# Weighing two heads instead of three on TensorE in most units of a mixture of softmaxes, with a new order of instructions

## The chip, the core and the metric

The kernel runs on one core of one Trainium2 chip. The metric is the device time of one execution in microseconds (us), lower is better. A core has five engines that run side by side, each working through its own instructions in order: TensorE (PE in the profile) multiplies matrices into PSUM, VectorE (DVE), ScalarE (ACT) and GpSimd (POOL) work on 128 partitions at a time, and SyncE (SP) here only issues DMAs. Sixteen DMA engines move data between HBM and SBUF.

## The reference: what is computed

```python
logits: (32, 128, 4 heads, 4096) float32; prior: (32, 128, 4) float32
prior_probs = softmax(prior, axis=-1)              # over the 4 heads
softmax     = softmax(logits, axis=-1)             # over the 4096 columns
mixture     = sum over heads of prior_probs * softmax   # (32, 128, 4096) float32
```

So 256 MiB are read, 64 MiB are written, and every logit is needed three times: for the maximum of its row, for the exponential and its sum, and for the weighted sum over the heads.

## The kernel before, in words

The work is cut into 32 **units** of 128 rows, one row to a partition. A unit has four heads of 128 x 4096 float32 (2 MB each). They are loaded into a **ring** of 11 slots of one head each (`slot`, line 104: head h of unit u sits in slot (4u + h) mod 11). A unit whose four heads run over the end of the ring is loaded by two DMAs, the others by one. The output is 2 MB a unit. It is put together in `obuf`, a single buffer, or from unit 24 on in some units in the slot of head 3 (`home`, line 107), and leaves from there.

Each step has a letter, and the order of the whole program is a hand-made text of such letters (`ORDER`), which `run` (line 193) turns into instructions. Each engine gets its instructions in that order and waits inside it; data dependencies between engines become semaphore waits. A word like `X0+1` means step X, argument 0, of the unit after the current one; `T12'` would be of the unit before; `@23` names the unit. Digits behind the head number are quarters of the 4096 columns: `12` is the second quarter (1024 columns), `24` the last two.

- `L` (`load`, line 112) and `S` (`store`, line 119): DMAs issued by SyncE, in one queue.
- `M` (`peak`, line 122, VectorE): minus the maximum of a head's rows.
- `E` (`exp`, line 127, ScalarE): the exponential in place, with the sum of each row.
- `R` (`recip`, line 133, VectorE): one over that sum.
- `G` (`diagonal`, line 136, GpSimd): the identity matrix times (one over the sum) times (prior weight), a 128 x 128 matrix.
- `X` (`weigh`, line 143, TensorE): that diagonal matrix times a head, added up in PSUM (`acc`, 4096 columns). A float32 block of 512 columns is two instructions in the trace, so a head is 16 of them.
- `C` (`weight`, line 152, GpSimd): the same weight as one number a row (`wght`).
- `Z` (`scale`, line 155, GpSimd): a head's columns times its weight, in place.
- `A`, `B`, `T` (`term`, line 162, VectorE): head times weight plus something else: plus `acc` into the output (`A`), plus `acc` into the head's own slot (`B`), head 3 plus what is in the slot of head 2 into the output (`T`, both from SBUF).
- `V` (`evac`, line 181, ScalarE): a quarter of `acc` copied into the slot of head 1.
- `P` (`add_scaled`, line 184, GpSimd): the slot of head 1 plus the slot of head 3, into the output.

In the **steady part** before (line 29, the first 23 entries of `ORDER`) TensorE weighs heads 0, 1 and 2 of each unit. Head 3 is finished in two ways: in the first half of the columns VectorE adds it to `acc` (`A01'`, `A12'`), in the second half ScalarE copies `acc` out (`V23'`, `V34'`), GpSimd scales head 3 (`Z324'`) and adds the two (`P23'`, `P34'`). These come behind the first maximum of the following unit. The store of a unit and the load two units further on are issued by SyncE after that, `S' L+2`. From unit 23 on an order of its own (lines 32 to 65) names every step of the **last units**, with heads split into quarters; there some quarters of head 2 are not weighed by TensorE (`BYPASS`, line 66) but scaled by GpSimd and added (`W`, line 177) to head 3.

What sets when a load can start is the ring: `L` of unit u+2 overwrites heads 1, 2 and 3 of unit u-1 and head 0 of unit u. What sets when a unit's output can be written is that the store of the unit before has left `obuf`.

Of the kernel before, what the change touches and what calls it, by code (L numbers as in the profile page):

```python
# [9 lines left out]
AF = mybir.ActivationFunctionType  # L10
# [12 lines left out]

FIRST = "L01 L12 L23 L34"
ORDER = []
ORDER += [
    "M0 E0 R3' C3' Z324' M1 R0 G0 A01' A12' V23' P23' V34' P34' E1 X0 S' L+2 M2 E2 R1 "
    "G1 X1 M3 E3 R2 G2 X2 "  # L30
] * 23
ORDER += [
    "M0@23 R3@22 E0@23 M2@23 Z324@22 C3@22 V34@22 R0@23 A12@22 G0@23 V23@22 P34@22 "
    "X034@23 E2@23 M1@23 X023@23 P23@22 X012@23 R2@23 E1@23 A01@22 G2@23 M3@23 X001@23 "
    "R1@23 E3@23 M1@24 G1@23 X123@23 S@22 X112@23 X101@23 M0@24 E1@24 L02@25 X201@23 "
    "X134@23 R3@23 E0@24 R1@24 Z324@23 M3@24 X234@23 X223@23 C3@23 G1@24 V34@23 X212@23 "
    "R0@24 V23@23 A01@23 P34@23 E3@24 A12@23 L24@25 G0@24 M2@24 P23@23 X034@24 X023@24 "
    "X012@24 M0@25 E2@24 X001@24 X101@24 S@23 R2@24 E0@25 R3@24 G2@24 X134@24 M1@25 "
    "Z324@24 X123@24 C3@24 X234@24 L02@26 R0@25 E1@25 M2@25 G0@25 X223@24 X112@24 "
    "V34@24 X201@24 M3@25 V23@24 P34@24 X212@24 E2@25 P23@24 X023@25 A01@24 L24@26 "  # L40
    "X034@25 E3@25 A12@24 X001@25 R2@25 R1@25 G2@25 M1@26 G1@25 X101@25 X012@25 X112@25 "
    "R3@25 E1@26 M0@26 Z324@25 X123@25 C3@25 S@24 X212@25 M2@26 E0@26 X201@25 X134@25 "
    "L02@27 X223@25 R0@26 E2@26 A12@25 G0@26 X234@25 A01@25 M3@26 X012@26 V23@25 "
    "X001@26 V34@25 P23@25 X034@26 R1@26 E3@26 P34@25 R2@26 L24@27 X023@26 M0@27 G1@26 "
    "G2@26 X123@26 X112@26 M1@27 E0@27 X134@26 X101@26 X201@26 S@25 R3@26 E1@27 R0@27 "
    "Z324@26 M2@27 X212@26 C3@26 G0@27 X223@26 L02@28 X234@26 V23@26 A01@26 E2@27 "
    "P23@26 X023@27 A12@26 M3@27 X012@27 V34@26 X001@27 P34@26 X034@27 R1@27 E3@27 "
    "R2@27 G1@27 Z234@27 X123@27 L24@28 G2@27 M0@28 X112@27 X101@27 X134@27 R3@27 E0@28 "
    "M1@28 C3@27 Z304@27 X202@27 S@26 V34@27 W34@27 X223@27 R0@28 E1@28 M2@28 G0@28 "
    "P34@27 X034@28 L01@29 V01@27 R1@28 M3@28 G1@28 E2@28 X001@28 P01@27 X101@28 L12@29 "  # L50
    "X134@28 V12@27 R2@28 Z224@28 M0@29 V23@27 X012@28 E3@28 P23@27 X023@28 L23@29 "
    "X112@28 P12@27 M1@29 E0@29 X123@28 G2@28 X201@28 L34@29 V23@28 X212@28 R0@29 R3@28 "
    "G0@29 M2@29 V34@28 Z314@28 X023@29 E1@29 X034@29 C3@28 S@27 W23@28 A01@28 E2@29 "
    "R1@29 X001@29 W34@28 M3@29 L01@30 G1@29 P23@28 X101@29 V12@28 R2@29 E3@29 X012@29 "
    "P12@28 X123@29 L12@30 G2@29 P34@28 X134@29 R3@29 M0@30 X201@29 V34@29 C3@29 "
    "Z304@29 X112@29 V01@29 L23@30 E0@30 X223@29 M1@30 Z234@29 X212@29 P01@29 L34@30 "
    "V23@29 R0@30 E1@30 G0@30 M2@30 P23@29 X001@30 X034@30 W34@29 L01@31 V12@29 X023@30 "
    "R1@30 E2@30 M3@30 G1@30 P12@29 X012@30 X101@30 P34@29 L12@31 X134@30 R2@30 E3@30 "
    "M0@31 G2@30 X123@30 Z234@30 X112@30 L23@31 V34@30 R3@30 E0@31 C3@30 X212@30 M1@31 "
    "Z314@30 X201@30 W34@30 L34@31 X223@30 V12@30 R0@31 A01@30 E1@31 G0@31 P12@30 "  # L60
    "X012@31 M2@31 X001@31 S@28 P34@30 V23@30 X034@31 R1@31 E2@31 M3@31 G1@31 P23@30 "
    "X023@31 X134@31 S@29 X123@31 R2@31 E3@31 G2@31 C2@31 B234@31 X101@31 B223@31 S@30 "
    "X201@31 R3@31 C3@31 T23@31 X112@31 T34@31 X212@31 A01@31 S23@31 A12@31 S34@31 "
    "S01@31 S12@31 "
]
BYPASS = {(27, 3), (28, 2), (28, 3), (29, 3), (30, 3), (31, 2), (31, 3)}


@with_exitstack
def kernel(  # L70
# [6 lines left out]
    nc = tc.nc  # L77
    U, P, H, V = logits.shape
# [4 lines left out]
    W = 512  # L83
    C = V // 4
# [11 lines left out]
    wght = cpool.tile([P, U, H], FP32, name="wght")  # L96
# [7 lines left out]
    def slot(u, h, a=0, b=4):  # L104
        return ring[:, (4 * u + h) % SLOTS, a * C : b * C]

    def home(u, a, b):
        if u >= U - 3 or u >= 24 and u % 2:
            return slot(u, 3, a, b)
        return obuf[:, a * C : b * C]  # L110
# [32 lines left out]
    def weigh(u, h, a=0, b=4):  # L143
        e = slot(u, h)
        for k in range(a * C // W, b * C // W):
            nc.tensor.matmul(  # L146
                acc[:, k * W : (k + 1) * W], lhsT=diag[:, u % 2, h],
                rhs=e[:, k * W : (k + 1) * W],
                start=h == 0, stop=h == H - 2 or (u, k * W // C) in BYPASS and h == H - 3,
            )  # L150

    def weight(u, h):
# [9 lines left out]
    def term(u, h, o, more, a, b):  # L162
        nc.vector.scalar_tensor_tensor(  # L163
            out=o, in0=slot(u, h, a, b), scalar=wght[:, u, h : h + 1], in1=more,
            op0=ALU.mult, op1=ALU.add,
        )
# [7 lines left out]
    def add_both(u, a, b):  # L174
        term(u, 3, home(u, a, b), slot(u, 2, a, b), a, b)

    def add_second(u, a, b):
        e = slot(u, 3, a, b)
        nc.gpsimd.tensor_add(e, e, slot(u, 2, a, b))  # L179

    def evac(u, a, b):
        nc.scalar.activation(slot(u, 1, a, b), acc[:, a * C : b * C], AF.Copy)  # L182
# [1 line left out]
    def add_scaled(u, a, b):  # L184
        nc.gpsimd.tensor_add(home(u, a, b), slot(u, 1, a, b), slot(u, 3, a, b))  # L185

    step = {
        "L": load, "S": store, "M": peak, "E": exp, "R": recip, "G": diagonal, "X": weigh,
        "C": weight, "Z": scale, "A": add_last, "B": add_head, "T": add_both, "V": evac,
        "P": add_scaled, "W": add_second,  # L190
    }

    def run(u, words):
        for w in words.split():
            op, digits, back, on, at = re.fullmatch(
                r"([A-Z])(\d*)('*)(?:\+(\d+))?(?:@(\d+))?", w
            ).groups()
            v = int(at) if at else u - len(back) + int(on or 0)
            if 0 <= v < U:
                step[op](v, *map(int, digits))  # L200

    with tc.manual_schedule():
        run(0, FIRST)
        nc.scalar.dma_start(out=pr, in_=prior)
        run(1, "L")

        nc.gpsimd.memset(ident, 1.0)
        nc.gpsimd.affine_select(
            out=ident, in_=ident, pattern=[[-1, P]], compare_op=ALU.is_equal, fill=0.0,
            base=0, channel_multiplier=1,  # L210
        )

        nc.vector.reduce_max(pmax, pr, axis=AX.X)  # L213
        nc.vector.tensor_sub(pr, pr, pmax.unsqueeze(2).to_broadcast([U, P, H]))  # L214
        nc.scalar.activation(pr, pr, AF.Exp)  # L215
        nc.vector.reduce_sum(pmax, pr, axis=AX.X)  # L216
        nc.vector.reciprocal(pmax, pmax)
        nc.vector.tensor_mul(  # L218
            pn.rearrange("k h r -> k r h"), pr, pmax.unsqueeze(2).to_broadcast([U, P, H])
        )  # L220
        for t in range(P // 32):
            nc.vector.transpose(  # L222
                pp[32 * t : 32 * (t + 1)], pn[:, :, 32 * t : 32 * (t + 1)]
            )

        for u, words in enumerate(ORDER):
            run(u, words)


# [28 lines left out]
```

## Time and profile before

| what | value |
|---|---|
| median of 3 runs | 787.25 us (786.92 to 787.46) |
| the profiled execution's own time | 787.27 us |
| its span (first to last instruction) | 785.5 us |
| granted TensorE clock, mean | 0.959 |
| DMA: bytes, mean rate | 335.89 MB, 428 GB/s |
| chain that ended last: DMA, PE, DVE | 50%, 29%, 12% |

The page gives for each engine its busy time and its share of the span, in a strip of 40 slices how busy it was over time, then the DMA queues, the chain of waits that ended last, and groups of equal instructions with their mean duration. A busy share of an engine says how much work it has; whether this work sets the time is told by what waited for what.

### The profile page before, as it was taken

The page shows a single profiled execution, that of the slowest core. Times are in us where ns is not written, and L with a number is a line of the kernel's source. Part 1 is how long each engine was busy: PE and PEld are TensorE (multiplying, and loading weights), DVE is VectorE, ACT ScalarE, POOL GpSimd, SP SyncE. Part 2 cuts the span into 40 slices and gives each one's busy share as a digit, 9 for nine tenths or more (in the row PEclk, how much of TensorE's full clock was granted, in tenths as well). Part 3 has the DMA queues.
Part 4 walks back from the last instruction along what each step waited for, and adds up shares of the span by engine and source line. Part 5 has one row for each costly group of instructions (what it writes and reads, how often), then busy time and mean ns, then how long its engine had stood idle before and what let it go on. Part 6 is the DMA issues. An engine that isn't in the chain of part 4 may idle for free.

```text
span 785.5 us, 4560 instructions
## 1 busy us (share of the span) xinstructions
PE 677.7 (86%) x1508; PEld 292.1 (37%) x1508; DVE 645.6 (82%) x327; ACT 549.1 (70%) x326; POOL 294.1 (37%) x243
## 2 busy tenths in 40 slices
PE   0959997979996989996899699799888999988896
PEld 0424443434442434342344244244333343433342
DVE  6489779877959777978795899577979988799796
ACT  2556758756866676875775868568668866879883
POOL 0032324432323323433332434134332433468981
PEclk9979999989998999998999799989999999999999
DMA  9999999999999999999999999999999999999997
GB/s 377 474 394 415 461 415 418 463 427 422 433 415 445 443 441 416 436 422 441 425 438 439 411 449 434 431 434 415 453 422 425 435 427 433 434 423 430 429 429 329
DMA packets 13030, 335.89 MB, mean 428 GB/s; under 512 B 1456, under 2 KB 1456, under 8 KB 2000
## 3 DMA queue, kind: packets, MB, share of 16 engines
q1 hardware_dynamic: 12960, 335.55, 99.5%
q8 instruction: 12, 0.20, 0.1%
q14 instruction: 10, 0.08, 0.0%
q10 hardware_dynamic: 48, 0.07, 0.0%
HBM read 268.50 MB, written 67.11 MB: 427 GB/s over the span
## 4 chain that ended last, share of the span: by engine, by line
DMA 50%; PE 29%; DVE 12%; ACT 3%; issue 3%; POOL 2%; SPq 0%; DVEq 0%; POOLq 0%
DMA ring<-in_logits_dram 48%; PE acc L146 29%; DVE nmax L123 11%; DMA out_dram<-ring 2%; ACT ring L128 2%; ACT ring L182 1%; POOL ring L185 1%; DVE obuf L163 1%; SPq L116 0%; POOL obuf L185 0%; POOL ring L157 0%; DVE rden L134 0%; POOL diag L137 0%; DVE ring L163 0%; SPq L120 0%
## 5 line engine op out<-in xcount | busy, mean ns | idle before, releaser
L146 PE MATMUL acc<-ring,diag 128*128 128x512 f32 x1508 | 677.7, 611 | 101.3 <-ACT ring L182 62.4
L123 DVE TENSOR_REDUCE nmax<-ring 128x1 f32<-128x4096 f32 x128 | 563.2, 4410 | 114.9 <-DMA ring<-in_logits_dram 114.9
L128 ACT ACTIVATE ring<-ring,nmax 128x4096 f32<-128x4096 f32 x128 | 474.8, 3710 | 200.1 <-DVE rden L134 94.4
L146 PEld LDWEIGHTS acc<-ring,diag 128*128 128x128 f32 x1508 | 292.1, 196 | 486.0 <-issue 357.9
L185 POOL TENSOR_TENSOR obuf<-ring 128x1024 f32<-128x1024 f32 x55 | 129.4, 2372 | 23.1 <-ACT ring L182 12.2
L137 POOL TENSOR_SCALAR diag<-ident,rden,pp 128x128 f32<-128x128 f32 x96 | 43.4, 452 | 226.8 <-DVE rden L134 218.6
L157 POOL TENSOR_SCALAR ring<-ring,rden,pp 128x2048 f32<-128x2048 f32 (+3 forms) x35 | 74.4, 2126 | 34.4 <-DVE rden L134 34.4
L182 ACT ACTIVATE ring<-acc 128x1024 f32<-128x1024 f32 x68 | 66.9, 1011 | 19.4 <-PE acc L146 19.4
L153 POOL TENSOR_TENSOR wght<-rden,pp 128x1 f32<-128x1 f32 x33 | 6.3, 192 | 191.0 <-DVE rden L134 191.0
L163 DVE SCALAR_TENSOR_TENSOR obuf<-ring,wght,acc 128x1024 f32<-128x1024 f32 x53 | 65.5, 1272 | 3.0 <-DMA out_dram<-obuf 2.0
L185 POOL TENSOR_TENSOR ring<-ring 128x1024 f32<-128x1024 f32 x13 | 30.6, 2369 | 4.2 <-issue 4.2
L134 DVE RECIPROCAL rden<-dsum 128x1 f32<-128x1 f32 x128 | 19.2, 155 | 8.4 <-ACT ring L128 8.4
L128 ACT ACTIVATION_READ_ACCUMULATOR ring<-ring,nmax 128x1 f32 x128 | 24.1, 188 | 0.0
L179 POOL TENSOR_TENSOR ring<-ring 128x1024 f32<-128x1024 f32 x5 | 11.8, 2366 | 0.2
L163 DVE SCALAR_TENSOR_TENSOR ring<-ring,wght,acc 128x1024 f32<-128x1024 f32 x7 | 8.8, 1275 | 2.0 <-PE acc L146 1.2
L213 DVE TENSOR_REDUCE pmax<-pr 32x128 f32<-32x512 f32 x1 | 0.7, 674 | 5.2 <-DMA pr<-in_prior_dram 5.2
L215 ACT ACTIVATE pr<-pr 32x512 f32<-32x512 f32 x1 | 0.6, 630 | 4.2 <-DVE pr L214 4.2
L163 DVE SCALAR_TENSOR_TENSOR ring<-ring,wght 128x1024 f32<-128x1024 f32 x2 | 2.5, 1280 | 0.3 <-POOL wght L153 0.3
L215 ACT ACT_TABLE_LOAD x1 | 1.3, 1283 | 1.2 <-PEq L242 1.2
L222 DVE STREAM_TRANSPOSE pp<-pn 32x128 f32<-32x128 f32 x4 | 1.2, 302 | 0.1
L216 DVE TENSOR_REDUCE pmax<-pr 32x128 f32<-32x512 f32 x1 | 0.7, 674 | 0.7 <-ACT pr L215 0.7
L218 DVE TENSOR_TENSOR pn<-pr,pmax 32x512 f32<-32x512 f32 x1 | 1.0, 1021 | 0.0
(8 smaller groups left out, 2.5 us busy)
## 6 DMA issues: line engine op xcount, KB each, us to landing
out_dram<-obuf SPq DMA_DIRECT2D x27, 2048.0 KB, 14.9
ring<-in_logits_dram SPq DMA_DIRECT2D x12, 4096.0 KB, 25.8
ring<-in_logits_dram SPq DMA_DIRECT2D x21, 2048.0 KB, 21.9
ring<-in_logits_dram SPq DMA_DIRECT2D x5, 6144.0 KB, 29.0
out_dram<-ring SPq DMA_DIRECT2D x4, 2048.0 KB, 14.2
out_dram<-ring SPq DMA_DIRECT2D x4, 512.0 KB, 5.0
ring<-in_logits_dram SPq DMA_DIRECT2D x17, 30.9
pr<-in_prior_dram ACTq DMA_DIRECT2D x1, 64.0 KB, 4.4
```

The lines of the kernel that those rows point to most:

```text
L123: nc.vector.tensor_reduce(out=nmax[:, u, h : h + 1], in_=slot(u, h), op=ALU.max, axis=AX.X, negate=True)
L128: nc.scalar.activation(slot(u, h), slot(u, h), AF.Exp, bias=nmax[:, u, h : h + 1], accum_out=dsum[:, u, h : h + 1],)
L134: nc.vector.reciprocal(rden[:, u, h : h + 1], dsum[:, u, h : h + 1])
L137: nc.gpsimd.tensor_scalar(out=diag[:, u % 2, h], in0=ident, scalar1=rden[:, u, h : h + 1], scalar2=pp[:, h, u : u + 1], op0=ALU.mult, op1= ...
L146: nc.tensor.matmul(acc[:, k * W : (k + 1) * W], lhsT=diag[:, u % 2, h], rhs=e[:, k * W : (k + 1) * W], start=h == 0, stop=h == H - 2 or (u ...
L153: nc.gpsimd.tensor_mul(wght[:, u, h : h + 1], rden[:, u, h : h + 1], pp[:, h, u : u + 1])
L157: nc.gpsimd.tensor_scalar(out=e, in0=e, scalar1=rden[:, u, h : h + 1], scalar2=pp[:, h, u : u + 1], op0=ALU.mult, op1=ALU.mult,)
L163: nc.vector.scalar_tensor_tensor(out=o, in0=slot(u, h, a, b), scalar=wght[:, u, h : h + 1], in1=more, op0=ALU.mult, op1=ALU.add,)
L179: nc.gpsimd.tensor_add(e, e, slot(u, 2, a, b))
L182: nc.scalar.activation(slot(u, 1, a, b), acc[:, a * C : b * C], AF.Copy)
L185: nc.gpsimd.tensor_add(home(u, a, b), slot(u, 1, a, b), slot(u, 3, a, b))
L215: nc.scalar.activation(pr, pr, AF.Exp)
```

## The change

In units 0 to 23 TensorE weighs heads 0 and 1 alone (16 instructions fewer a unit, and one `G` fewer). Heads 2 and 3 are added by the other engines, quarter by quarter:

- Quarter 0: VectorE puts head 2 times its weight plus `acc` into the slot of head 2 (`B201`), then adds head 3 times its weight, into the output (`T01`).
- Quarter 1: ScalarE copies `acc` out (`V12`), GpSimd scales head 2 (part of `Z214`) and adds the copy to it (`N12`), VectorE adds head 3 times its weight (`T12`).
- Quarters 2 and 3: ScalarE copies `acc` out (`V23`, `V34`) and scales head 3 (`Y324`, new); GpSimd scales head 2 (the rest of `Z214`), adds the copy (`N23`, `N34`) and adds head 3 into the output (`I23`, `I34`, new).

A unit so has one `C` more (`C2`), three `N` and two `I` in place of two `P`, one `V` more, two `T` and one `B` in place of two `A`. The order of the steady part is new: a unit's first two maxima and first exponential stand in the entry before, and its sums are finished in the entry behind its last exponential. The number of loads and stores, their sizes and their order in SyncE's queue are as before. In units 24 to 31 the mix of steps is nearly that of before (`N` and `I` take the place of `W` and of five `P`, `A` is 9 instead of 10 and `V` 21 instead of 20); their order is new from unit 20 on.

```diff
+STEADY = (
+    "S' R0+1 C3 T12 Y324 N23 E1+1 G0+1 T01 M2+1 I23 R1+1 {} I34 G1+1 M3+1 E2+1 R2+1 "
+    "E3+1 X0+1 C2+1 X1+1 V12+1 Z214+1 B201+1 V23+1 V34+1 M0+2 N12+1 R3+1 N34+1 E0+2 "
+    "M1+2 "
+)
+ORDER = [STEADY.format("")] * 2 + [STEADY.format("L+2")] * 21
 ORDER += [
-    "M0 E0 R3' C3' Z324' M1 R0 G0 A01' A12' V23' P23' V34' P34' E1 X0 S' L+2 M2 E2 R1 "
-    "G1 X1 M3 E3 R2 G2 X2 "
-] * 23
...
+    "X001@31 R1@31 M3@31 G1@31 I34@30 X123@31 S@29 X134@31 R2@31 E3@31 G2@31 C2@31 "
+    "B223@31 X112@31 B234@31 S@30 X101@31 R3@31 C3@31 T23@31 X201@31 T34@31 X212@31 "
+    "A01@31 S23@31 A12@31 S34@31 S01@31 S12@31 "
 ]
-BYPASS = {(27, 3), (28, 2), (28, 3), (29, 3), (30, 3), (31, 2), (31, 3)}
+
+BY_PE = {24: 4, 25: 4, 26: 4, 27: 3, 28: 2, 29: 3, 30: 3, 31: 2}
...
-                start=h == 0, stop=h == H - 2 or (u, k * W // C) in BYPASS and h == H - 3,
+                start=h == 0, stop=h == H - 2 or h == H - 3 and k * W // C >= BY_PE.get(u, 0),
...
+    def scale_act(u, h, a, b):
+        e = slot(u, h, a, b)
+        nc.scalar.activation(e, e, AF.Copy, scale=wght[:, u, h : h + 1])
+
     def add_second(u, a, b):
-        e = slot(u, 3, a, b)
-        nc.gpsimd.tensor_add(e, e, slot(u, 2, a, b))
+        e = slot(u, 2, a, b)
+        nc.gpsimd.tensor_add(e, e, slot(u, 1, a, b))
+
+    def add_third(u, a, b):
+        nc.gpsimd.tensor_add(home(u, a, b), slot(u, 2, a, b), slot(u, 3, a, b))
...
-        "C": weight, "Z": scale, "A": add_last, "B": add_head, "T": add_both, "V": evac,
-        "P": add_scaled, "W": add_second,
+        "C": weight, "Z": scale, "Y": scale_act, "A": add_last, "B": add_head, "T": add_both,
+        "V": evac, "P": add_scaled, "N": add_second, "I": add_third,
...
-        for u, words in enumerate(ORDER):
+        for u, words in enumerate(ORDER, -2):
             run(u, words)
```

The second argument of `enumerate` starts the entries at unit -2, so that the first two bring unit 0 and unit 1 under way.

## The prediction, on record before the change was run

> **What bounds the kernel now.** First the page: whose time is full?
>
> ```profile
> span 785.5 us, 4560 instructions
> PE 677.7 (86%) x1508; PEld 292.1 (37%) x1508; DVE 645.6 (82%) x327; ACT 549.1 (70%) x326; POOL 294.1 (37%) x243
> DMA  9999999999999999999999999999999999999997
> q1 hardware_dynamic: 12960, 335.55, 99.5%
> ```
>
> No engine is full, but the one queue of loads and stores keeps its 16 DMA engines busy for 99.5% of the span, in every slice but the last. The chain of waits then seems to speak for TensorE too (29% of the span):
>
> ```profile
> 196.70 27.72 PE acc L146 x64
> 224.45 0.04 issue
> 224.49 34.88 DMA ring<-in_logits_dram
> 259.39 4.42 DVE nmax L123
> ```
>
> A load is issued when a head has been weighed and lands 34.88 us later. That is no transfer time: in the trace's packets, 64 KB take 2.418 us and 16 KB 0.611 us in the median, so 8 MB over 16 engines take 8 x 2.418 = 19.3 us. The other 15.5 us the load stood in a queue. The timeline shows the same of the store and load that follow:
>
> ```profile
> 249.35 0.34 SPq L120 DMA_DIRECT2D out_dram<-obuf  x1
> 254.82 0.33 SPq L116 DMA_DIRECT2D ring<-in_logits_dram  x1
> 259.39 4.42 DVE L123 TENSOR_REDUCE nmax<-ring 128x1 f32<-128x4096 f32 x1 [4.19 <-DMA ring<-in_logits_dram]
> ```
>
> The store is issued 10.0 us before the load ahead of it lands (259.4). Over the whole trace the stores of units 1 to 27 are issued 7.6 to 13.3 us before the transfer ahead of them lands, loads behind the start mostly over 9, at least 4.7; only behind the last load is it less (3 to 6 us), and there too landings follow each other without a gap, 4.85 us a store, up to 784.46. So **the queue is the bound**, from the first landing to the last.
>
> What could be won? One unit moves at least 8 x (2.418 + 0.611) = 24.23 us; landings in the chain lie 24.2 us a unit apart (259.4 to 525.6, 11 units). All packets at their median durations come to 778.9 us an engine; those of the trace to 782.5. So 3.6 us of stretched packets are all that a better fed queue can give back: 0.6 in the first 5 us, 0.8 between 55 and 65 us, the rest in crumbs. The span's own ends (some 2 us to the first packet, 1.4 behind the last) stay.
>
> **The change, part by part.** The profiled execution took 787.27 us (span 785.5 and 1.8 around it), the median is 787.25; sums are made against 787.27.
>
> DMAs: the same sizes in the same order, so 778.9 us stays. The question is only whether steps are done in time to issue them. I work out one steady unit v, from zero where its load lands; u is the unit before. Rows:
>
> ```profile
> 245.48 23.00 PE L146 MATMUL acc<-ring,diag 128*128 128x512 f32 x48 [7.34 <-ACT ring L182]
> 269.79 20.84 PE L146 MATMUL acc<-ring,diag 128*128 128x512 f32 x48 [1.31 <-ACT ring L182]
> 268.18 2.46 DVE L163 SCALAR_TENSOR_TENSOR obuf<-ring,wght,acc 128x1024 f32<-128x1024 f32 x2
> 716.45 2.90 POOL L157 TENSOR_SCALAR ring<-ring,rden,pp 128x3072 f32<-128x3072 f32 x1
> L185 POOL TENSOR_TENSOR obuf<-ring 128x1024 f32<-128x1024 f32 x55 | 129.4, 2372 | 23.1 <-ACT ring L182 12.2
> L163 DVE SCALAR_TENSOR_TENSOR ring<-ring,wght 128x1024 f32<-128x1024 f32 x2 | 2.5, 1280 | 0.3 <-POOL wght L153 0.3
> ```
>
> - VectorE: a maximum with its reciprocal starts every 4.40 us, a quarter's add every 1.19 (268.18, next step at 270.55). M0(v) 0 to 4.4, M1 to 8.8, R0 8.9, `T12` and `T01` of u to 11.2, M2 to 15.6, M3 to 20.0, R2. The two-input adds `T` cost 1.28 in the row that has them; work rises from 20.0 (4 x 4.40 and two adds) to 21.2 us a unit.
> - ScalarE: E0 4.5 to 8.2, `Y324` to 10.1, E1 to 13.8, E2 15.6 to 19.4 (waits for M2), E3 20.0 to 23.8, three `V` of 0.92 to 26.6. `Y324` has no row: not below half an exponential (3.71/2), as two `V` 1.92, not above a full exponential, and even then E1 ends at 15.5, before it is needed. I take 1.9.
> - TensorE: G0 starts 0.2 us behind R0, so 9.05 to 9.5. The head's 16 instructions at 0.43 are 6.9 us. TensorE has then been idle for some 8 us; the two PE rows above show the price: 2.2 us more behind 7.34 us of idleness than behind 1.31 (seven such starts in the trace: 1.5 to 3.1). X0 9.55 to 18.65, X1 to 25.5, its first quarter at 20.4.
> - `B201` behind that quarter: 20.5 to 21.7. Then VectorE is free, **2.5 us before the next landing at 24.23**; 1.6 at the dearest cold start.
> - GpSimd: C2 20.2, `Z214` 2.90 to 23.3, `N12` (behind V12) 24.9 to 27.2, `N34` 29.6, C3, `N23` to 32.1, which is 7.9 of the next unit; G0, then `I23` behind `Y324` 10.3 to 12.6, `I34` to 15.0, G1 at 15.7. Adds by the 2.37 of L185, 2.35 start to start. 15.9 us of work a unit.
> - SyncE: S(u) at 15.1, L(v+2) behind X0 at 18.7. The load ahead lands at 24.23 and S(u) at 29.1, so they are issued 9.1 and 10.4 us ahead: as in before. `T12` writes `obuf`, so VectorE waits there for the store before; it landed at 4.9, needed at 8.8.
>
> All engines hold the 24.23: the longest ring of waits (G0, X0, X1, `V34`, `N34`, C3, `N23`, G0) is 0.5 + 9.1 + 6.9 + 1.1 + 2.6 + 0.2 + 2.4 = 22.8 us. So the whole saving on TensorE (24 x 6.9 us less work) buys nothing, since no transfer waited for it, and the added work (24 x 1.2 us on VectorE, 24 x 2.8 on ScalarE, 24 x 7.7 on GpSimd) costs nothing while it fits under the transfers; if that cover were gone, each microsecond over 24.23 would cost some 22.
>
> Start: with L1 landing at 42.3, S(0) is issued at 42.3 + 15.1 = 57.4 (before 56.5) and L3 at 61.0 (before 62.8), 5.0 and 6.5 us ahead (before 5.9 and 4.7): the 0.8 us of stretch there may shrink or stay. End: the last loads set M of unit 30 and 31; in before the chain runs through 84 instructions of TensorE from 740.91 to 778.94, the last add, the last store. Unit 30 and 31 keep these 84, and their first waits on the same landing, so the end moves by a cold start more or less: -1.5 to +1.2. Sum: 787.27 - 0.3 (part of the start's stretch) +- 1.3: **787.0**, 785.9 to 788.6. Measurements of this kernel can tell about 0.2% (1.6 us) from no change; so this is no change.
>
> [...] No row has a VectorE add of two SBUF inputs beside GpSimd work; the two in the trace run while GpSimd is idle. [...]
>
> **The rivals.**
> 1. *`T12` and `T01` wait for GpSimd's adds, and VectorE becomes the bound* (slower). Below, a T loses nothing; above, a whole add, 2.35. [...] It decides from 2.5 us of waits a unit. If `I23` gets in ahead of `T01` (2.35 + 0.45 with G0), everything up to `N23` moves back, and that holds up the next `T12` by 1.5 or so: 25.9 us a unit, 1.7 x 22 = 37 less the 9 us that stand queued: 787 + 28 = 815. If both wait a whole add: 26.4, 826. For it: VectorE has least room. Against: only these two steps of a unit are exposed. 0.14.
> 2. *The new order of the last units lets the queue run short* (slower). Place: one store or load from unit 22 on that is issued later than 3 us before the landing ahead of it; each further microsecond is one of the end. Before, the least lead there up to unit 27 was 8.5, so a step must come 5.5 us later to cost anything; a step that slips behind one more head (6.9 and a cold start, 2.2) costs 3.6, two such 13: 789 to 800. For it: every word there is moved. Against: same steps, and TensorE enters with less undone. 0.15.
> 3. *TensorE stays at half clock* through X0, 16 x 0.855 = 13.7: B201 ends at 26.3, 2.1 over, 787 + 2.1 x 22 - 9 = 824. The trace never shows more than 8 slow ones. 0.02.
> 4. *The stretch goes*: up to 3.6 us, 783.7 to 785.6. That would need nearly all crumbs. 0.07.
>
> That the change doesn't do what it says is hardly open: TensorE must show 1508 - 24 x 16 = 1124 instructions, VectorE 24 adds more.
>
> **The numbers.** Forecast 0.62, rivals 0.14, 0.15, 0.02, 0.07. Faster by over 0.2% is rival 4; slower rivals 1 to 3, 0.31. The range takes the forecast and rival 2, 785.6 to 798; outside lie rivals 1 and 3 and most of 4, some 0.2.
>
> **What would show it.** The DMA strip at 9 throughout and q1 at 99%; L163 at 1.28 for the new adds (2 or more, or idle time ahead of them put down to GpSimd, is rival 1); maxima that wait for the load in the steady part (if they wait for nothing, VectorE is the bound); slow matmuls at each X0, 5 to 8 of 16; SyncE's stores about 9 us ahead. Wrong if a slice of the DMA strip before the last falls under 9.

## The result and the profile after

The changed kernel takes 790.82 us (median of 12 runs, 787.82 to 796.44); the kernel before takes 787.38 us (12 runs, 786.92 to 788.28). The ratio is 1.0045, 95% interval 1.0025 to 1.0065: **slower by 0.45%**, where no change was forecast. It also spreads over 8.6 us, where the kernel before spreads over 1.4. The profiled execution took 791.51 us with a span of 789.6, 4.1 us more than before. Its page answers to the lines shown of before:

```profile
span 789.6 us, 3916 instructions
PE 540.9 (68%) x1124; PEld 230.3 (29%) x1124; DVE 688.6 (87%) x350; ACT 619.5 (78%) x375; POOL 524.6 (66%) x316
DMA  9999999999999999999999999999999999999997
q1 hardware_dynamic: 12960, 335.55, 99.3%
```

TensorE has its 1124 instructions, and no engine is full. The DMA strip looks as before, at 9 in every slice but the last. So the strip is too coarse to show where 4 us went. The packets show it. Call *stretch* the time that packets took beyond the median of their size, and *idle* the time in which a DMA engine had no packet, both divided by the 16 engines (for the whole run, from the first packet to the last):

| window, us | before: stretch + idle | after: stretch + idle |
|---|---|---|
| 50 to 70 (first store) | 0.84 + 0.00 | 0.32 + 0.08 |
| 70 to 590 (steady part) | 1.38 + 0.00 | 3.51 + 0.19 |
| 590 to 655 | 0.16 + 0.00 | 1.69 + 0.47 |
| whole run, first packet to last | 3.58 + 2.87 | 6.63 + 3.97 |

The sums differ by 4.15 us, the spans by 4.1: **the whole loss is in packets that take longer and in small gaps of the queue**, 2.3 us of it in the steady part and 2.0 at the beginning of the last units. This says where the time went, not yet why.

The groups tell what changed for the engines. The columns behind the bar are busy time, mean ns of one, and idle time before with what ended it. The first line is of the kernel before, the others are of the changed kernel:

```profile
L137 POOL TENSOR_SCALAR diag<-ident,rden,pp 128x128 f32<-128x128 f32 x96 | 43.4, 452 | 226.8 <-DVE rden L134 218.6
L142 POOL TENSOR_SCALAR diag<-ident,rden,pp 128x128 f32<-128x128 f32 x72 | 79.2, 1100 | 59.7 <-DVE rden L139 56.9
L191 POOL TENSOR_TENSOR obuf<-ring 128x1024 f32<-128x1024 f32 x50 | 116.9, 2356 | 0.0
L168 DVE SCALAR_TENSOR_TENSOR obuf<-ring,wght 128x1024 f32<-128x1024 f32 x48 | 74.0, 1578 | 0.2 <-issue 0.2
```

The diagonal matrices took 452 ns before, now 1100 in the mean. The new two-input adds of VectorE take 1578 instead of 1280. GpSimd's own adds (L191) are unchanged, 2356 against 2372. One steady unit in the timeline shows why (these lines are of the changed kernel):

```profile
223.22 15.45 PE L151 MATMUL acc<-ring,diag 128*128 128x512 f32 x32 [8.46 <-POOL diag L142]
238.70 1.02 ACT L194 ACTIVATE ring<-acc 128x1024 f32<-128x1024 f32 x1 [0.69 <-PE acc L151]
239.80 2.36 POOL L188 TENSOR_TENSOR ring<-ring 128x1024 f32<-128x1024 f32 x1 [0.82 <-ACT ring L194]
242.12 0.18 POOL L158 TENSOR_TENSOR wght<-rden,pp 128x1 f32<-128x1 f32 x1
242.27 2.35 POOL L188 TENSOR_TENSOR ring<-ring 128x1024 f32<-128x1024 f32 x1
244.29 2.61 DVE L168 SCALAR_TENSOR_TENSOR obuf<-ring,wght 128x1024 f32<-128x1024 f32 x2
244.61 2.45 POOL L142 TENSOR_SCALAR diag<-ident,rden,pp 128x128 f32<-128x128 f32 x1
247.12 5.14 PE L151 MATMUL acc<-ring,diag 128*128 128x512 f32 x8 [8.46 <-POOL diag L142]
```

Read it as a ring: both heads on TensorE (15.45), `V34` on ScalarE, `N34`, C3 and `N23` on GpSimd to 244.62, then `T12` and `T01` on VectorE to 246.90. G0, ready since 244.6, ends only at 247.06, just behind the second add: 2.45 us for what takes 0.45. Then TensorE starts on the next unit. One turn is 247.12 - 223.22 = **23.90 us**, of which 1.55 is the *cold start* in TensorE's 15.45: behind 8.46 us of rest its first matmuls take 0.85 us each instead of 0.43, while 32 at 0.43 and the pipeline are 13.9 (in experiment 4 they take 14.00). The granted clock shows it too, 0.868 in the mean against 0.959 before. Without the cold start a turn is 22.35. The DMA queue needs 24.23, at the packets' median durations. TensorE's starts in the chain of waits show that the cold start varies:

```profile
103.24 15.72 PE acc L151 x32
...
127.41 15.58 PE acc L151 x32
...
271.57 16.88 PE acc L151 x32
...
296.88 16.17 PE acc L151 x32
```

Over the whole steady part it costs 1.5 to 3.1 us a unit, so a turn takes 23.9 to 25.4 us, on either side of 24.23. From unit 0 to unit 21 starts lie 24.34 us apart in the mean (53.88 to 565.02). So the engines no longer run ahead. Stores 1 to 21 were issued 10.7 us ahead of the landing before them in the mean (7.6 to 13.3), now 7.1 (5.0 to 8.4). Loads 4 to 23 were 12.8 us ahead, now 8.6. One store of the changed kernel, with the landing before it told by the maximum that waits for it, 7.6 us later:

```profile
227.84 0.34 SPq L125 DMA_DIRECT2D out_dram<-obuf  x1
...
235.50 4.42 DVE L128 TENSOR_REDUCE nmax<-ring 128x1 f32<-128x4096 f32 x1 [0.60 <-DMA ring<-in_logits_dram]
```

### The profile page after: what moved, and what is told of

Its sections match the earlier page's. It is cut to its first block, busy times and chain, and to the rows that moved or that the text cites. A ratio compares the mean times of both kernels' runs of the same rounds, so it can differ in the third digit from the quotient of the medians.

```text
span 789.6 us, 3916 instructions
## 1 busy us (share of the span) xinstructions
PE 540.9 (68%) x1124; PEld 230.3 (29%) x1124; DVE 688.6 (87%) x350; ACT 619.5 (78%) x375; POOL 524.6 (66%) x316
## 4 chain that ended last, share of the span: by engine, by line
PE 43%; DMA 26%; ACT 12%; DVE 8%; issue 5%; POOL 5%; SPq 0%; POOLq 0%; ACTq 0%; DVEq 0%
PE acc L151 43%; DMA ring<-in_logits_dram 26%; ACT ring L133 7%; DVE nmax L128 7%; ACT ring L184 4%; POOL diag L142 4%; DVE obuf L168 1%; ACT ring L194 0%; DVE ring L168 0%; POOL ring L197 0%; POOL obuf L197 0%; SPq L121 0%; DVE rden L139 0%; POOLq L191 0%; SPq L125 0%
## 5 line engine op out<-in xcount | busy, mean ns | idle before, releaser
L151 PE MATMUL acc<-ring,diag 128*128 128x512 f32 x1124 | 540.9, 643 | 242.2 <-POOL diag L142 239.2
L128 DVE TENSOR_REDUCE nmax<-ring 128x1 f32<-128x4096 f32 x128 | 562.7, 4405 | 25.9 <-DMA ring<-in_logits_dram 25.9
L151 PEld LDWEIGHTS acc<-ring,diag 128*128 128x128 f32 x1124 | 230.3, 208 | 552.0 <-issue 279.3
L188 POOL TENSOR_TENSOR ring<-ring 128x1024 f32<-128x1024 f32 x77 | 181.6, 2359 | 71.1 <-ACT ring L194 65.2
L194 ACT ACTIVATE ring<-acc 128x1024 f32<-128x1024 f32 x93 | 94.0, 1017 | 42.4 <-PE acc L151 42.1
L142 POOL TENSOR_SCALAR diag<-ident,rden,pp 128x128 f32<-128x128 f32 x72 | 79.2, 1100 | 59.7 <-DVE rden L139 56.9
L191 POOL TENSOR_TENSOR obuf<-ring 128x1024 f32<-128x1024 f32 x50 | 116.9, 2356 | 0.0
L162 POOL TENSOR_SCALAR ring<-ring,rden,pp 128x3072 f32<-128x3072 f32 (+3 forms) x35 | 95.5, 2730 | 9.2 <-DVE rden L139 9.2
L168 DVE SCALAR_TENSOR_TENSOR ring<-ring,wght,acc 128x1024 f32<-128x1024 f32 x31 | 39.6, 1279 | 55.9 <-PE acc L151 55.1
L158 POOL TENSOR_TENSOR wght<-rden,pp 128x1 f32<-128x1 f32 x57 | 10.7, 188 | 101.1 <-DVE rden L139 101.1
L168 DVE SCALAR_TENSOR_TENSOR obuf<-ring,wght 128x1024 f32<-128x1024 f32 x48 | 74.0, 1578 | 0.2 <-issue 0.2
L184 ACT ACTIVATE ring<-ring,wght 128x2048 f32<-128x2048 f32 x24 | 47.7, 1990 | 0.0
L197 POOL TENSOR_TENSOR ring<-ring 128x1024 f32<-128x1024 f32 x10 | 23.6, 2373 | 7.9 <-issue 7.1
L191 POOL TENSOR_TENSOR ring<-ring 128x1024 f32<-128x1024 f32 x3 | 7.1, 2367 | 0.1
L168 DVE SCALAR_TENSOR_TENSOR obuf<-ring,wght,acc 128x1024 f32<-128x1024 f32 x4 | 5.0, 1273 | 0.4 <-POOL wght L158 0.4
```

The source lines that it names most:

```text
L128: nc.vector.tensor_reduce(out=nmax[:, u, h : h + 1], in_=slot(u, h), op=ALU.max, axis=AX.X, negate=True)
L142: nc.gpsimd.tensor_scalar(out=diag[:, u % 2, h], in0=ident, scalar1=rden[:, u, h : h + 1], scalar2=pp[:, h, u : u + 1], op0=ALU.mult, op1= ...
L151: nc.tensor.matmul(acc[:, k * W : (k + 1) * W], lhsT=diag[:, u % 2, h], rhs=e[:, k * W : (k + 1) * W], start=h == 0, stop=h == H - 2 or h ...
L162: nc.gpsimd.tensor_scalar(out=e, in0=e, scalar1=rden[:, u, h : h + 1], scalar2=pp[:, h, u : u + 1], op0=ALU.mult, op1=ALU.mult,)
L168: nc.vector.scalar_tensor_tensor(out=o, in0=slot(u, h, a, b), scalar=wght[:, u, h : h + 1], in1=more, op0=ALU.mult, op1=ALU.add,)
L184: nc.scalar.activation(e, e, AF.Copy, scale=wght[:, u, h : h + 1])
```

## The experiments

The first theory (A): the ring with its cold start sets how far ahead stores and loads stand, and a short lead stretches packets, long before the queue runs dry. The rival (B): the added traffic of three engines stretches the packets, whatever the lead. The expectations write "lead" for the time from an issue to the landing before it.

**1. Seven idle products on TensorE** between a unit's second head and the next unit's first:

```diff
+    def warm(u):
+        for _ in range(7):
+            nc.tensor.matmul(acc[:, 0:W], lhsT=ident, rhs=blank, start=True, stop=True)
...
-    "E3+1 X0+1 C2+1 X1+1 ...
+    "E3+1 K+1 X0+1 C2+1 X1+1 ...
```

> The changed kernel with seven idle products of the identity with a block of ones put on TensorE between the second head of one unit and the first head of the next, in units 0 to 23; they fill a part of PSUM that the first head then overwrites, so the result stays. Theory A (the ring X0, X1, V34, N34, C3, N23, T12, T01, G0 of 22.4 us and a cold start of 1.5 to 3.1 us sets the pace of the steady units, which eats the lead of the stores and loads, and short leads stretch packets): TensorE starts each X0 at full clock, the ring falls to 22.4, starts of X0 lie 24.2 us apart with the landings, stores are issued 7 to 8 us ahead without the dips to 5, stretch falls from 6.6 to about 4.5 us, 788 to 789 us with little spread. Theory B (the added traffic of VectorE, ScalarE and GpSimd in SBUF stretches the packets, whatever the lead): no change, 790 to 791 us.

Measured: 789.22 us (787.26 to 790.44), ratio 1.0015 (1.0005 to 1.0024). The means did not do what they should: TensorE still rested 2.5 us ahead of X0 and mostly began it cold again (1.6 to 1.8 us), leads stayed at 7.1 and 8.6. Yet the steady part lost 2.2 us against 3.7. Experiment 4 has more products.

**2. `T12` and `T01` behind the third maximum:**

```diff
-    "S' R0+1 C3 T12 Y324 N23 E1+1 G0+1 T01 M2+1 I23 ...
+    "S' R0+1 C3 Y324 N23 E1+1 G0+1 M2+1 T12 T01 I23 ...
```

> The changed kernel with T12 and T01 put behind the third maximum in the steady part, so that G0 finds VectorE in a maximum instead of in a two-input add. Theory A: G0 takes 0.45 us again instead of 2.45, X0 starts 2 us earlier behind its reciprocal, the ring (G0, X0, X1, V34, N34, C3, N23) falls to 21 to 23 us, under 24.2, and the pace is that of the landings; T12 and T01 now wait for I34 or hold it, so stores stand only 5 to 7 us ahead, loads 10; 788 to 789. Theory B: 790 to 791, since the traffic is the same.

Measured: 788.85 us (787.46 to 796.05), ratio 1.0027 (1.0006 to 1.0049).

```profile
342.00 0.45 POOL L142 TENSOR_SCALAR diag<-ident,rden,pp 128x128 f32<-128x128 f32 x1
342.41 4.70 POOL L191 TENSOR_TENSOR obuf<-ring 128x1024 f32<-128x1024 f32 x2
342.50 15.86 PE L151 MATMUL acc<-ring,diag 128*128 128x512 f32 x32 [8.18 <-POOL diag L142]
344.67 4.72 DVE L168 SCALAR_TENSOR_TENSOR obuf<-ring,wght 128x1024 f32<-128x1024 f32 x2
```

G0 takes 0.45 us again, and TensorE starts at once. Now `T12` and `T01` pay: 4.72 us for the two instead of 2.46, and their end is that of `I34` (347.1) plus the two. Loads stand 10.0 us ahead, stores 6.9, the steady part loses 3.0 us. The interval still overlaps that of the changed kernel, so a gain from this alone is not shown.

**3. The kernel before, with its store issued later.** Nothing of the change is in it; one add of GpSimd is moved, and the issue of the store and of the load with it:

```diff
-    "M0 E0 R3' C3' Z324' M1 R0 G0 A01' A12' V23' P23' V34' P34' E1 X0 S' L+2 M2 E2 R1 "
-    "G1 X1 M3 E3 R2 G2 X2 "
+    "M0 E0 R3' C3' Z324' M1 R0 G0 A01' A12' V23' P23' V34' E1 X0 M2 E2 R1 "
+    "G1 P34' S' L+2 X1 M3 E3 R2 G2 X2 "
```

> The kernel before with one add of GpSimd (P34) moved behind the second diagonal matrix in the steady part, so that each store is issued some 4.5 us later; nothing else is changed. Theory A: stores stand about 5.5 us ahead of the landing before them instead of 10, the stretch of packets rises from 3.6 to 5 or 6 us, 788.5 to 790 us. Theory B: the traffic is the same, so is the time, 787.4 us.

Measured: 797.54 us (797.12 to 798.11), ratio **1.0125 (1.0109 to 1.0140)**, more than either expected.

```profile
352.30 0.34 SPq L120 DMA_DIRECT2D out_dram<-obuf  x1
352.81 0.33 SPq L116 DMA_DIRECT2D ring<-in_logits_dram  x1
...
361.69 4.42 DVE L123 TENSOR_REDUCE nmax<-ring 128x1 f32<-128x4096 f32 x1 [8.01 <-DMA ring<-in_logits_dram]
...
380.33 0.34 SPq L120 DMA_DIRECT2D out_dram<-obuf  x1
380.78 1.29 SPq L116 DMA_DIRECT2D ring<-in_logits_dram  x2
...
385.91 4.42 DVE L123 TENSOR_REDUCE nmax<-ring 128x1 f32<-128x4096 f32 x1 [4.19 <-DMA ring<-in_logits_dram]
```

The second store is issued 5.6 us ahead of the landing at 385.9; 16 of the 21 stores stand so (5.5 to 6.4). The queue is hardly ever empty (0.35 us idle from 70 to 590 us), yet packets there stretch by 9.5 us instead of 1.4. Added traffic is not needed for that: its amount is that of the kernel before.

But the stretch does not sit where theory A puts it. The first store above is one of five that still stand 9.4 to 10.8 us ahead, and from its issue to the next store packets stretch by 1.10 us, more than behind any other of the 21. Behind these five it is 0.83 us each, behind the 16 with the short lead 0.33; in the kernel before it is 0.07. So issuing store and load later costs time here, but the lead of the single store is not what sets the price.

**4. Ten idle products.**

> As the kernel with seven idle products, but with ten of them, 8.6 us, so that TensorE does not rest 2.6 us ahead of X0. Theory A (the ring with its cold start sets the lead): X0 without slow matmuls, ring 22.4 us, pace 24.2 us of the landings, loads 10 to 12 us ahead, stores 7 to 8; 787.5 to 789, little spread. If the cold starts did not matter: as with seven products, 789.2.

Measured: 787.63 us (787.08 to 790.17), ratio 1.0012 (1.0002 to 1.0021), with the changed kernel's adds, their waits and the last units untouched.

```profile
341.88 14.00 PE L152 MATMUL acc<-ring,diag 128*128 128x512 f32 x32 [0.39 <-POOL diag L143]
...
355.72 8.75 PE L160 MATMUL acc<-blank,ident 128*128 128x512 f32 x20
```

A unit's two heads take 14.00 us instead of 15.5 to 16.9: no cold start in most units (a few landings still let TensorE rest). Loads stand 11.0 us ahead, stores 8.2, the steady part loses 1.8 us (before: 1.4), and from 590 to 655 us the loss is 0.3 instead of 2.2. So the order of the last units does not cost these 2 us by itself: they all but go when the steady part is less late. And theory B does not explain the loss of the changed kernel, since the added traffic is all there.

**5. Ten idle products and the later adds together.**

> The ten idle products and T12 and T01 behind the third maximum together. Theory A: neither GpSimd's G0 nor a cold start is left in the ring (20.5 us), the steady part runs at the pace of the landings with stores 6.5 to 7.5 us and loads 11 to 12 us ahead; what is left against the kernel before is the shorter lead of the stores and the last units: 788 to 789.

Measured: 790.54 us (790.04 to 791.88), ratio 1.0046 (1.0031 to 1.0061). A miss: the two cures together are worse than the first alone. Loads stand 11.4 us ahead, but stores 7.0 instead of 8.2; the steady part loses 2.6 us and 590 to 655 another 1.2. Longer leads of the loads do not help here; the shorter leads of the stores may be what costs, which is not shown.

**6 and 7. The kernel before with marks in SyncE's queue**, a DMA of 4 bytes ahead of each store and each load, which waits for a number that is there early (control) or late:

```diff
+    def mark_store(u):
+        nc.sync.dma_start(out=mark[0:1, 2 * u : 2 * u + 1], in_=nmax[0:1, u, 3:4])
+
+    def mark_load(u):
+        nc.sync.dma_start(out=mark[0:1, 2 * u + 1 : 2 * u + 2], in_=dsum[0:1, u, 3:4])
...
-    "M0 E0 R3' C3' Z324' M1 R0 G0 A01' A12' V23' P23' V34' P34' E1 X0 S' L+2 M2 E2 R1 "
-    "G1 X1 M3 E3 R2 G2 X2 "
+    "M0 E0 R3' C3' Z324' M1 R0 G0 A01' A12' V23' P23' V34' P34' E1 X0 M2 E2 R1 "
+    "G1 X1 M3 E3 J S' K L+2 R2 G2 X2 "
```

> The kernel before with a DMA of one number (4 bytes) put into SyncE's queue ahead of each store and ahead of each load of the steady part; here both wait for the first maximum of the unit, which is long done, so they delay nothing. It is the control of the next run. All theories: 787.4 to 788 us, stores about 10 us ahead, the load 3 to 6 us behind the store.

Measured: 787.06 us, ratio 0.9999 (0.9989 to 1.0009). The marks cost nothing.

> As the run before, but the number ahead of the store is the unit's fourth maximum, the one ahead of the load the sum of its fourth exponential, so that the store is issued some 4 us ahead of the landing before it instead of 10, and the load some 4 us behind the store. Theory A1 (what stretches packets is a short lead of the stores): as in the kernel with the late add, 5 to 10 us slower than the control, 793 to 798. Theory A2 (what stretches them is that a store and the next load are issued within half a microsecond of each other, as in the kernel with the late add): 0 to 2 us slower than the control.

Measured: 810.72 us, ratio 1.0298 (1.0282 to 1.0313). 15 of 21 stores stand 3.5 to 5.6 us ahead, five 8.5 to 9.1, the load 4 us behind the store; 14.8 us more stretch and 8.6 more idle than before. So it is not enough that store and load are apart; A2 falls. A1 has the direction, but as in experiment 3 the stretch is larger behind the five stores that stand far ahead (1.3 us each) than behind the others (0.5). (With so late a load the engines wait for landings too, so the sum is not the price of the lead alone.)

**8. G0 made by VectorE**, right behind its reciprocal, so that it cannot wait behind the adds:

```diff
+    def diagonal_dve(u, h):
+        nc.vector.tensor_scalar(
+            out=diag[:, u % 2, h], in0=ident, scalar1=rden[:, u, h : h + 1],
+            scalar2=pp[:, h, u : u + 1], op0=ALU.mult, op1=ALU.mult,
+        )
...
-    "S' R0+1 C3 T12 Y324 N23 E1+1 G0+1 T01 ...
+    "S' R0+1 D0+1 C3 T12 Y324 N23 E1+1 T01 ...
```

> The changed kernel with the diagonal matrix of head 0 made by VectorE itself, right behind its reciprocal and ahead of T12, in units 0 to 23, so that it waits for no add; T12 and T01 stay where they are. Theory A (G0 held by the two adds puts 2 us and the adds themselves into the ring): X0 starts some 0.5 us behind the reciprocal instead of 2.9, the ring no longer passes VectorE's adds, units come at the landings' 24.2 us although cold starts stay, loads 10 us or more ahead, stores 8: 787.5 to 788.5 us. If the hold of G0 did not matter: 790 to 791.

Measured: 810.40 us (809.39 to 810.75), ratio 1.0288 (1.0273 to 1.0304): the largest miss, and the clearest sight of how much longer adds of VectorE and GpSimd take beside each other (in the mean 2257 ns for VectorE's instead of 1280, 3118 for `I23` and `I34` instead of 2356).

```profile
353.02 2.35 POOL L194 TENSOR_TENSOR ring<-ring 128x1024 f32<-128x1024 f32 x1
...
353.85 1.60 DVE L149 TENSOR_SCALAR diag<-ident,rden,pp 128x128 f32<-128x128 f32 x1
355.38 4.57 DVE L174 SCALAR_TENSOR_TENSOR obuf<-ring,wght 128x1024 f32<-128x1024 f32 x2
...
355.64 6.52 POOL L197 TENSOR_TENSOR obuf<-ring 128x1024 f32<-128x1024 f32 x2 [0.27 <-POOL ring L194]
```

The diagonal matrix takes 1.60 us and ends at 355.45, just behind `N23` (355.37). Then `I23`, no longer behind G0, gets in ahead of `T01`: the two adds take 4.57 us instead of 2.46, and `I23` and `I34` 6.52 instead of 4.68. VectorE becomes the bound: TensorE's starts lie 25.3 us apart, stores stand 2.0 us ahead. That is the first rival of the prediction, which it put at 25.9 us and 815.

**9. A longer ring:** the first quarter of head 0 weighed twice.

```diff
+    def twice(u):
+        for k in range(2):
+            nc.tensor.matmul(
+                acc[:, k * W : (k + 1) * W], lhsT=diag[:, u % 2, 0],
+                rhs=slot(u, 0)[:, k * W : (k + 1) * W], start=True, stop=True,
+            )
...
-    "E3+1 X0+1 C2+1 ...
+    "E3+1 K+1 X0+1 C2+1 ...
```

> The changed kernel with the first quarter of head 0 weighed twice in units 0 to 23 (the first time it is overwritten), 1.7 us more on TensorE in the ring; busy time of TensorE stays far under that of the kernel before. Theory A: ring 22.4 + 1.5 to 3.1 + 1.7 = 25.6 to 27.2 us, over 24.2, so the steady units come at the pace of the ring: 1.4 to 2.5 us a unit late, 787 + 30 to 50 less 5 that stand queued = 812 to 832 us. If TensorE has room (its busy share is 68%): 791.

Measured: 839.42 us (839.21 to 839.56), ratio 1.0659 (1.0641 to 1.0676). Starts lie 26.7 us apart in the mean (53.91 to 614.32), inside the expected 25.6 to 27.2: 1.7 us more on TensorE, whose share is far from full, pass into every unit (24.34 to 26.7). The sum of 812 to 832 was too small: it took off lead that was not there and left out the stretch. The DMA strip now shows gaps:

```profile
DMA  9999999899799989998999997999999999999998
```

## Why the prediction was wrong

*The bound* was read rightly: DMA is the bound, and the less work on TensorE bought nothing. *The added work under the transfers*: the durations without waits were right (`Y324` 1.99 for 1.9, `Z214` 2.90, adds 2.36), and ScalarE's work grew by 70 us for the 67 of 24 x 2.8. VectorE's grew by 43 us instead of 29 and GpSimd's by 230 instead of 185; what is over is waits (VectorE has 23 adds more, not 24: the last units have one less).

*The step that failed first* is the one on GpSimd and the ring: "G0 starts 0.2 us behind R0, so 9.05 to 9.5". G0 does not get in between the two adds; it ends just behind both, after 2.45 us instead of 0.45, so 2.0 us late. That joins VectorE's adds to the ring, which is then not 22.8 us but 23.9 to 25.4 with the cold start as it fell out. Experiment 9 shows that the ring passes its length on, experiment 4 takes the cold start out and brings the time to within 0.12% (0.02 to 0.21%) of before. What the hold of G0 costs by itself is not shown: experiment 2 takes it away, but its interval overlaps that of the changed kernel, and with it on top of experiment 4 (experiment 5) the time is longer than with 4 alone.

*The step that failed second* is in what bounds the kernel: I took a store issued 3 us ahead of the landing before it as early enough, from the last stores of the kernel before, and so priced a later issue at nothing ("costs nothing while it fits under the transfers"). Experiment 3 shows that it is not free: the kernel before with 16 of 21 stores 5.5 to 6.4 us ahead, and the queue idle for only 0.35 us, loses 1.25%. The same wrong limit stands in rival 2, which needed "5.5 us later to cost anything". Its place was nearly right: store 22 stands 5.4 us ahead in the changed kernel and from 590 to 655 us 2.0 of the 4.1 us are lost.

*Luck*: 790.82 us lies in the range of 785.6 to 798 only because rival 2 was taken into it. The forecast's own part, 785.9 to 788.6, does not hold it (and by its sum it should read 785.7 to 788.3, 1.3 on both sides of 787.0). Rival 2 gave the last units' order as the reason; the larger part of the loss, 2.3 us, lies in the steady part, which the forecast put at nothing. The sign of being wrong, a slice of the DMA strip under 9, did not come, for the strip does not show 4 us; the signs that did come are stores 7.1 us ahead instead of about 9, and new adds at 1.58 us instead of 1.28.

*Rival 1* had the direction of the hold: the new adds and GpSimd's work take longer beside each other. The runs show it: G0 2.45 us instead of 0.45 (the changed kernel), the two adds 4.57 (experiment 8) and 4.72 (experiment 2) instead of 2.46. Its wait of a whole add, 2.35 us, was my estimate (the length of one of GpSimd's adds) and no run shows it for each of the two; experiments 2 and 8 show 2.1 to 2.3 us more for the two together. But in the changed kernel the price falls on the other engine than I put it: VectorE's adds take only 0.3 us more each (1578 against 1280 ns), GpSimd's G0 2.0.

*Open*: what in the DMA engines stretches a packet when transfers are issued later. It is not the mean lead alone: the changed kernel loses 3.7 us in its steady part with stores 7.1 us ahead, experiment 3 loses 9.9 with 6.9, experiment 5 loses 2.6 with 7.0. It is not the lead of the single store, by experiments 3 and 7. In experiment 3 a store and the next load are issued within half a microsecond, but so they are in most units of experiment 5, where little stretches, and experiment 7 shows that this is not needed. What the traces do show is the place: of the steady part's stretch, 3.2 of 3.5 us in the changed kernel and 7.8 of 9.5 in experiment 3 fall on packets that start within 5 us behind an issue of SyncE, and these are 57% and 31% of the packets. Nor is it settled why G0 stands behind both adds of VectorE, while `I23` in experiment 8 stands behind one.

## What to carry to other kernels

In a kernel whose DMA engines are busy throughout, look not only whether the queue ever runs dry but also at what packets take beyond their median, and at how many microseconds ahead each transfer is issued. Transfers issued later cost time here long before the queue was empty (experiment 3: 1.25%, with the queue idle for 0.35 us of the steady part); how much, no rule from these runs tells. Add up every ring of waits that closes over a unit, with cold starts at their dearest (3.1 us here) and with VectorE's adds of two SBUF inputs and GpSimd's work in a row (here G0 took 2.45 us instead of 0.45), and compare it with the DMA's time for a unit (24.23 us here): TensorE, busy for 68% of the changed kernel, still set the pace when it had 1.7 us more a unit (experiment 9: starts 26.7 us apart instead of 24.34). No version of the change beats the kernel before; the nearest, experiment 4, only wins back most of what the change had lost.

## What the runs showed of the hardware

What TensorE's cold start costs differs from start to start. In the changed kernel TensorE rests 8.5 us in most units, and the start costs (beyond 13.9 us for the 32 matmuls) 3.0 us after a disturbance, then 2.3, 1.9, 1.7, 1.6 over the next units, down to 1.54, where the turns stay at 23.90 us until a landing disturbs them. The granted clock in its trace goes with that: it is 0.50 from the start at 223.22 us to 226.1 and 1.00 from 226.3 to 243.1, and behind the dearer start at 271.57 it is 0.50 to 277.3 and 1.00 from 277.5 to 290.9. What sets how long it stays at 0.50 was not shown. In experiment 9, at some 27 us a turn, the cost goes round: 1.5, 2.4, 2.8, 3.0, 3.1, 3.2 and 1.5 again. Experiment 1 has a cold start of 1.6 to 1.8 us behind 2.5 us of rest. That the spread of 8.6 us comes from the cold starts was not shown by itself, though it shrinks to 3.1 us with the ten products that keep TensorE busy (experiment 4).
